# Down and output projections as three 256-column matmuls, with new starting places for weights, memory, x and latents

## The chip, the core and the metric

The kernel runs on one core of one Trainium2 chip. The metric is the device time of one execution in microseconds (us). Before the change it is 1103.97 us, the median of 3 runs (1102.92 to 1104.38).

## What is computed

A trunk of two layers over 256 tokens of width 1024 in float32. Every layer adds to x, in turn, half of a feed-forward network (FFN, width 2816), a mixer, a cross-attention to a memory of 256 tokens, and half of a second FFN. The mixer of the first layer is a differential attention beside a stick-breaking attention (called AB below), that of the second is a latent attention with a low-rank key, value and query (MLA).

```python
def swiglu(h, w_gate, w_up, w_down):
    return (jax.nn.silu(h @ w_gate) * (h @ w_up)) @ w_down
...
        x = x + 0.5 * swiglu(rms_norm(x, ffn_norm[layer, 0]),
                             ffn_w_gate[layer, 0], ffn_w_up[layer, 0], ffn_w_down[layer, 0])
...
            x = x + diff_stickbreak_mixer(h, ab_w_in[i], ab_w_out[i], ...)
...
            x = x + mla_mixer(h, mla_w_dq[i], mla_q_norm[i], mla_w_uq[i], mla_w_dkv[i], ...)
        x = x + memory_cross_attention(rms_norm(x, xm_norm[layer]), rms_norm(mem, xm_mem_norm[layer]), ...)
        x = x + 0.5 * swiglu(rms_norm(x, ffn_norm[layer, 1]), ...)
```

## The kernel before

Every large product is made of numbers that are split in two float32r parts, a high and a low one: high times high, high times low and low times high are added up in one PSUM bank. A matmul of TensorE holds 128x128 numbers (the held operand, loaded by a weight load) and streams the columns of the other operand past them (the streamed operand). In the profile's names `mm<-xh,wh` the first name behind the arrow is the streamed operand, the second the held one.

**Triples and pairs.** `mm3` (line 286) makes a step of 128 rows as three matmuls, lines 287, 288 and 289. `mm2` (line 279) makes it as two: line 282 streams the high and the low part, which lie side by side, as 512 columns past the weight's high part, and line 283 streams the 256 high columns past the weight's low part. The two halves of the bank are then added to x one after the other in `finish_dt` (lines 518 to 520).

```python
        PE.matmul(bank[:, 0:512], w[0], src[2], start=first, stop=False)
        PE.matmul(bank[:, S:512], w[1], src[0], start=False, stop=last)
```

**Which product is which.** Gate and up products (`fm`, line 618), the query projections of the cross-attention, the first projections of MLA and `qb`, `kb` of AB (`fm_g`, line 628) stream x past the weights, as triples. `ka`, `qa`, `va`, `vb` of AB and the memory's keys and values (`tm_g`, line 641) hold x or the memory and stream the weights, as triples of 256 columns; so do `kv_product` (line 1380, 512 columns) and `q_product` (line 1395, 384 columns), which hold the latents. The down products of the FFN (`ffn`, lines 734 to 744) and the output projections of the mixers and the cross-attentions (`out_g`, line 663) are pairs.

**Places.** All sizes of tiles are multiples of 128 bytes. Where an operand starts inside its tile is counted in words of 4 bytes: `COLUMNS` = 28 (112 bytes) and `ROWS` = 36 (144 bytes, 16 past a multiple of 128). x starts at 28 in every stage but AB, where it starts at 36 (`X_AT`, line 72); the hidden activations, the sources of the output projections and the latents at 28 (the slots of the arena, line 185, handed out as a `Pair` of two blocks with a high and a low part each); the memory at 36 (line 790); the weights, loaded in chunks of up to 128x2048, at 0 (line 229).

**Order of the work.** TensorE's order is written by the program itself. In the FFNs it is the order of the loops. In mixers and cross-attentions a planner (`run`, line 438) with estimated times (`spend`, `drop`, `signal`) picks which attention step stands between which pieces of the projections; a product gives way after every 4 steps (lines 635 and 649). A weight chunk is loaded by a DMA on SP's queue, rounded to its high part by ScalarE (line 244), and the low part is subtracted by VectorE, in the mixers a quarter of it by GpSimd (line 246). Three chunks have room (`HL`), so the next chunk's rounding waits until TensorE has left the buffer. The order on the other engines is a scheduler's.

Of the kernel before, what the change touches and what calls it, by code (L numbers as in the profile page):

```python
# [19 lines left out]
P = 128  # L20
S = 256
# [31 lines left out]
WTIME = 4.41  # L53
SLOTS_MLA = (29, 12)
AB_ORDER = ('ka', 'qa', 'vb', 'va', 'k0', 'k1', 'v0')
# [13 lines left out]

COLUMNS, ROWS = 28, 36  # L70

X_AT = (COLUMNS, ROWS) + 7 * (COLUMNS,)
SLOTS_MIX = (29, 12)

# [85 lines left out]
def trunk_kernel(ctx, tc, wflat, xT_d, xtok_d, memT_d, memtok_d, gains_d, rows_d, cst_d, out_d):  # L160
# [109 lines left out]
    def weight(key, n):  # L270
# [6 lines left out]
        return (hi[:, :w].rearrange("p (k n) -> p k n", n=n), lo[:, :w].rearrange("p (k n) -> p k n", n=n))  # L277

    def mm2(bank, w, src, first, last):


        PE.matmul(bank[:, 0:512], w[0], src[2], start=first, stop=False)  # L282
        PE.matmul(bank[:, S:512], w[1], src[0], start=False, stop=last)  # L283
        spend(0.231 + 0.118)

# [203 lines left out]

    class Pair:  # L490


        def __init__(self):
            self.t = alloc("r")
            self.v = self.t.rearrange("p (q h s) -> p q h s", h=2, s=S)
            self.h, self.l = self.v[:, :, 0, :], self.v[:, :, 1, :]
            self.blocks = [(self.v[:, q, 0, :], self.v[:, q, 1, :], self.t[:, q * 512:(q + 1) * 512])
                           for q in range(2)]

# [163 lines left out]
    def out_g(keyf, nchunk, groups, gc):  # L663
# [5 lines left out]
        def part(dt, g):  # L669
# [3 lines left out]
            for i, k in enumerate(rows_):  # L673
                mm2(pss[dt], (w[0][:, k, j * P:(j + 1) * P], w[1][:, k, j * P:(j + 1) * P]),
                    src[i], g == 0 and i == 0, g == len(groups) - 1 and i == len(rows_) - 1)
            if g == len(groups) - 1:
                left[dt // per] -= 1
                if not left[dt // per]:
                    done(keyf(dt // per))
                ps = pss.pop(dt)  # L680
                finish_dt(dt, gc, ps)
                drop(ps, 1.2)

# [12 lines left out]
    def ffn(l, j, gc, need_rb, mem=None):  # L696
# [4 lines left out]
        for f in range(FT // 2):  # L701
# [23 lines left out]
            V.tensor_tensor(out=u, in0=u, in1=s, op=ALU.mult)  # L725
            h = Pair()
            split1(h.h, h.l, u.rearrange("p (a b) -> p a b", b=S))
            rel(u, s)
            tiles.append(h.t)
            hs += h.blocks  # L730
            if mem is not None and f in MEM_AT:
                mem_gain(mem, MEM_AT.index(f))
        begin_phase()
        for dp in range(4):
            pss = [ps_("mm"), ps_("mm")]
            for g0, gn in FF_GROUPS:
                w = weight(("down", l, j, dp, g0), 256)
                for q in range(2):
                    for i in range(gn):
                        k = g0 + i  # L740
                        mm2(pss[q], (w[0][:, i, q * P:(q + 1) * P], w[1][:, i, q * P:(q + 1) * P]),
                            hs[k], k == 0, k == FT - 1)
            for q in range(2):
                finish_dt(dp * 2 + q, gc, pss[q], 0.5)
        rel(*tiles)
# [115 lines left out]
    def cross(l, gc):  # L861
# [32 lines left out]
        def attend(hp):  # L894
# [28 lines left out]
            rel(*pT)  # L923
            h = Pair()
            split1(h.h, h.l, po.rearrange("p (a b) -> p a b", b=S))
            tiles.append(h.t)
            srcs[hp] += h.blocks
            drop(po, 1.3)
# [24 lines left out]
    def mixer_ab(gc):  # L953
# [7 lines left out]

        def add_src(i, h):
            tiles.append(h.t)
            srcs[i] += h.blocks

# [77 lines left out]
        def stick(hq, g):  # L1043
# [12 lines left out]
            for z in zs:  # L1056
# [8 lines left out]
                rel(e)  # L1065
                pr = Pair().t
                split1(pr[:, 0:384], pr[:, 512:896], sp[:, 0:384])
                sps.append((sp, pr))
            for i, (z, (sp, pr)) in enumerate(zip(zs, sps)):
                yield dict(lat=EST_AB['st2'] if i else EST_AB['st1'])  # L1070
                for o in (0, 512):
                    PE.matmul(z[:, 0:384], ntri, pr[:, o:o + 384], start=False, stop=False, skip_group_check=True)
                PE.matmul(z[:, P:S], nones, sp[:, S:384], start=False, stop=True, skip_group_check=True)
# [5 lines left out]
                ws.append(w_)  # L1079
                rel(sp, pr)  # L1080
            yield dict(lat=EST_AB['sto'], o=1 - g, after=[ev["vb", hq]] + [ev["po", hq]] * g)
# [10 lines left out]
            if g == 1:  # L1092
                h = Pair()
                split1(h.h, h.l, po.rearrange("p (a b) -> p a b", b=S))
                add_src(hq, h)
                drop(po, 1.3)
# [94 lines left out]
        def turn_o(g):  # L1191
            yield dict(t=1, after=[ev["oa", t] for t in range(2)])
            pt = transpose4([oa[t][:, (2 * g + j) * P:(2 * g + j + 1) * P] for j in range(2) for t in range(2)])
            h = Pair()
            split(h.h, h.l, pt.rearrange("p (a b) -> p a b", b=S), gsub)
            add_src(2 + g, h)
            drop(pt, 1.4)
# [11 lines left out]
    def mixer_mla(gc):  # L1209
        xg, rs = st.xg, st.rs  # L1210
        ev = defaultdict(Event)
        lat_tiles, tiles, srcs = [], [], [[] for _ in range(4)]
        lat = {"ckv": ([], []), "cq": ([], [])}
        rl, kk, kf, vt, kT, qf, rqs = {}, {}, {}, {}, {}, {}, {}

        def latent(key, gc0, ps):
            pairs, sqs = lat[key]
            h = Pair()
            for j in range(2):
                split(h.blocks[j][0], h.blocks[j][1], ps[:, j * S:(j + 1) * S], gcol(gc0 + j))  # L1220
            pairs += h.blocks
            lat_tiles.append(h.t)
            sq = al()
# [156 lines left out]
        def kv_product(hf):  # L1380
            yield dict(w=("ukv", hf))
            w = weight(("ukv", hf), 1024)
            for t in range(2):
                yield dict(mm=2)
                pk, pv = take("mm"), take("mm")
                for pz, c0 in ((pk, 0), (pv, 512)):
                    for k in range(2):
                        mm3(pz, tuple(z[:, t * P:(t + 1) * P] for z in lat["ckv"][0][k][:2]),
                            (w[0][:, k, c0:c0 + 512], w[1][:, k, c0:c0 + 512]), k == 0, k == 1)
# [17 lines left out]
        def attend(n):  # L1407
# [57 lines left out]
            rel(*pT)  # L1465
            h = Pair()
            split1(h.h, h.l, po.rearrange("p (a b) -> p a b", b=S))
            tiles.append(h.t)
            srcs[n] += h.blocks
            drop(po, 1.3)  # L1470
# [126 lines left out]
```

## Time and profile before

| what | value |
|---|---|
| median of 3 runs (lowest to highest) | 1103.97 us (1102.92 to 1104.38) |
| the profiled execution: its time, its span | 1103.84 us, 1102.1 us |
| TensorE: matmuls, weight loads (busy, share of the span) | 1079.7 us (98%), 1019.4 us (92%) |
| VectorE, ScalarE, GpSimd busy | 793.3 us (72%), 654.9 us (59%), 196.1 us (18%) |
| mean granted clock of TensorE | 0.995 |
| DMA queue of the weights | 191.86 MB, 50.4% of 16 engines |

Matmuls follow each other in a pipeline: one that is listed with 0.28 us may be followed by the next 0.11 us later, so what a matmul costs is read from the distance of two starts, not from its duration. The profile's span runs from the first to the last instruction; the time holds 1.74 us more.

### The profile page before, as it was taken

How to read it: one execution, taken by the hardware profiler on the slowest of the kernel's cores; microseconds unless marked ns; L12 is line 12 of the kernel's file. 1: busy time of each engine (PE TensorE's matmuls, PEld its weight loads, DVE VectorE, ACT ScalarE, POOL GpSimd, SP SyncE). 2: the span in 40 equal slices, each digit the busy share in tenths (PEclk: the TensorE clock that was granted, in tenths of full speed). 3: DMA queues.
4: the chain of work that ended last, by engine and by line, in shares of the span. 5: the costliest groups of instructions: out<-in, count | busy, mean ns of one | idle time of the engine just before them, and what ended most of it. 6: DMA issues, size and time to landing. Idle time of an engine off the chain costs nothing.

```text
span 1102.1 us, 21671 instructions
## 1 busy us (share of the span) xinstructions
PE 1079.7 (98%) x8144; PEld 1019.4 (92%) x8144; DVE 793.3 (72%) x1930; ACT 654.9 (59%) x1775; POOL 196.1 (18%) x210
## 2 busy tenths in 40 slices
PE   8999999999999999999999999999989999999998
PEld 8999988998889899998899999889878899999987
DVE  6888766667877878775777777665678768877653
ACT  6666555576756666554556655565866556655541
POOL 2000001366344200000100000114861422000000
PEclk9999999999999999999999999999989999999999
DMA  8766555535236165545556555554241443655561
GB/s 296 250 236 207 186 172 195 189 106 175 97 123 218 71 229 200 192 182 194 185 183 233 196 207 182 175 190 162 96 138 54 153 146 124 230 193 190 193 218 49
DMA packets 50794, 193.25 MB, mean 175 GB/s; under 512 B 5760, under 2 KB 7552, under 8 KB 35584
## 3 DMA queue, kind: packets, MB, share of 16 engines
q1 hardware_dynamic: 50688, 191.86, 50.4%
q8 instruction: 64, 1.05, 0.4%
q14 instruction: 42, 0.34, 0.1%
HBM read 190.79 MB, written 1.05 MB: 174 GB/s over the span
## 4 chain that ended last, share of the span: by engine, by line
PE 87%; DVE 6%; ACT 3%; POOL 2%; issue 1%; DMA 1%; SPq 0%; DVEq 0%; ACTq 0%; POOLq 0%
PE mm L282 19%; PE mm L287 18%; PE mm L288 18%; PE mm L289 18%; PE mm L283 10%; DVE wl L246 2%; ACT slotf L763 1%; PE t L776 1%; POOL sm L468 1%; PE s L1428 1%; DMA wr<-wflat 1%; PE t L476 1%; PE s L901 0%; PE o L1461 0%; DMA gains<-gains 0%
## 5 line engine op out<-in xcount | busy, mean ns | idle before, releaser
L244 ACT CAST wh<-wr 128x256 fp32r<-128x256 f32 (+1 forms) x1216 | 441.0, 434 | 303.9 <-PE mm L288 141.5
L246 DVE TENSOR_TENSOR wl<-wr,wh 128x256 fp32r<-128x256 f32 (+1 forms) x1171 | 483.6, 466 | 122.5 <-ACT wh L244 111.5
L287 PE MATMUL mm<-xh,wh 128*128 128x256 f32 x1584 | 439.6, 278 | 4.1 <-DVE slotf L715 2.0
L289 PE MATMUL mm<-xh,wl 128*128 128x256 f32 x1584 | 437.6, 276 | 0.1
L288 PE MATMUL mm<-xl,wh 128*128 128x256 f32 x1584 | 437.3, 276 | 0.2 <-DVE xl L483 0.2
L282 PE MATMUL mm<-slotr,wh 128*128 128x512 f32 x896 | 318.3, 398 | 1.1 <-DVE slotr L483 1.1
L287 PEld LDWEIGHTS mm<-xh,wh 128*128 128x128 f32 x1584 | 298.2, 188 | 5.3 <-issue 2.2
L288 PEld LDWEIGHTS mm<-xl,wh 128*128 128x128 f32 x1584 | 298.1, 188 | 0.5 <-DVE xl L483 0.4
L289 PEld LDWEIGHTS mm<-xh,wl 128*128 128x128 f32 x1584 | 298.1, 188 | 0.5 <-DVE wl L267 0.3
L283 PE MATMUL mm<-slotr,wl 128*128 128x256 f32 x896 | 252.2, 281 | 0.0
L282 PEld LDWEIGHTS mm<-slotr,wh 128*128 128x128 f32 x896 | 168.3, 188 | 42.8 <-DVE slotr L483 1.4
L283 PEld LDWEIGHTS mm<-slotr,wl 128*128 128x128 f32 x896 | 168.8, 188 | 0.1
L540 POOL TENSOR_TENSOR acc<-acc,sq 128x256 f32<-128x256 f32 x49 | 42.9, 875 | 462.4 <-ACT sq L532 458.5
L246 POOL TENSOR_TENSOR wl<-wr,wh 128x512 fp32r<-128x512 f32 x45 | 66.8, 1485 | 108.6 <-ACT wh L244 108.6
L723 DVE TENSOR_TENSOR slotf<-mm,rb 128x512 f32<-128x512 f32 x44 | 30.3, 689 | 52.7 <-PE mm L289 52.6
L519 DVE SCALAR_TENSOR_TENSOR x<-mm,x 128x256 f32<-128x256 f32 x128 | 52.1, 416 | 21.4 <-PE mm L283 21.0
L482 ACT ACTIVATE xh<-x,gains 128x256 fp32r<-128x256 f32 x64 | 32.1, 507 | 33.9 <-DVE x L519 29.5
L763 ACT ACTIVATE slotf<-s,sm,sl 128x256 f32<-128x256 f32 (+1 forms) x64 | 32.8, 522 | 23.3 <-DVE sm L757 17.8
L715 DVE TENSOR_TENSOR slotf<-mm,rb 128x512 f32<-128x512 f32 x44 | 30.3, 688 | 20.9 <-PE mm L289 20.8
L483 DVE SCALAR_TENSOR_TENSOR xl<-x,gains,xh 128x256 fp32r<-128x256 f32 x64 | 39.2, 617 | 5.2 <-ACT xh L482 5.2
L287 PE MATMUL mm<-wh,mem 128*128 128x256 f32 x128 | 38.0, 297 | 0.0
L488 DVE TENSOR_TENSOR slotr<-slotf,slotr 128x512 fp32r<-128x512 f32 (+1 forms) x52 | 35.5, 686 | 3.2 <-ACT slotr L487 2.9
(194 smaller groups left out, 1085.5 us busy)
## 6 DMA issues: line engine op xcount, KB each, us to landing
wr<-wflat SPq DMA_DIRECT2D x118, 1024.0 KB, 4.8
wr<-wflat SPq DMA_DIRECT2D x180, 256.0 KB, 3.9
wr<-wflat SPq DMA_DIRECT2D x16, 768.0 KB, 4.4
slotf<-memT SPq DMA_DIRECT2D x8, 256.0 KB, 3.5
x<-xT SPq DMA_DIRECT2D x4, 256.0 KB, 5.1
wr<-wflat SPq DMA_DIRECT2D x2, 512.0 KB, 7.2
slotf<-xtok SPq DMA_DIRECT2D x4, 256.0 KB, 7.6
slotf<-memtok SPq DMA_DIRECT2D x4, 256.0 KB, 3.5
```

The source lines that it names most:

```text
L244: A.copy(hi[:, a:b], raw[:, a:b])
L246: e.tensor_tensor(out=lo[:, a:b], in0=raw[:, a:b], in1=hi[:, a:b].bitcast(F32), op=ALU.subtract)
L282: PE.matmul(bank[:, 0:512], w[0], src[2], start=first, stop=False)
L283: PE.matmul(bank[:, S:512], w[1], src[0], start=False, stop=last)
L287: PE.matmul(out, a[0], b[0], start=first, stop=False, **kw)
L288: PE.matmul(out, a[0], b[1], start=False, stop=False, **kw)
L289: PE.matmul(out, a[1], b[0], start=False, stop=last, **kw)
L483: V.scalar_tensor_tensor(out=lo, in0=src, scalar=g, in1=hi.bitcast(F32), op0=ALU.mult, op1=ALU.subtract))
L488: V.tensor_tensor(out=lo, in0=src, in1=hi.bitcast(F32), op=ALU.subtract)
L519: V.scalar_tensor_tensor(out=xd, in0=ps[:, h * S:(h + 1) * S], scalar=factor, in1=xd, op0=ALU.mult, op1=ALU.add)
L540: G.tensor_tensor(out=st.acc, in0=st.acc, in1=sq, op=ALU.add)
L763: A.activation(p[:, i * w:(i + 1) * w], sps[:, i * w:(i + 1) * w], AF.Exp, bias=nb[:, i:i + 1], scale=r, accum_out=sums[:, i:i + 1])
```

## The change

Three things are done together.

1. `mm2` and `Pair` are gone: down products and output projections are made by `mm3`, from a high and a low part that lie in two slots of 512 words, into 256 columns of a bank. `finish_dt` adds one block to x instead of two.
2. Where the weights are streamed, they start at 28 instead of 0, and what is held (x in AB, the memory, the latents) starts at 0 instead of 36 or 28. In `qb` and `kb`, where x of AB is streamed, x is at 0 instead of 36 and the weights at 56 (224 bytes) instead of 0. All weight buffers get 64 words more.
3. The arenas of the two mixers have 11 slots of 512 words in place of 6 pairs of two. The latents take the first 6.

```diff
-COLUMNS, ROWS = 28, 36
-X_AT = (COLUMNS, ROWS) + 7 * (COLUMNS,)
-SLOTS_MIX = (29, 12)
+COLUMNS = 28
+X_AT = (COLUMNS, 0) + 7 * (COLUMNS,)
+W_COLUMNS = {"ka": 28, "qa": 28, "va": 28, "vb": 28, "memk0": 28, "memv0": 28, "memk1": 28, "memv1": 28,
+             "uq": 28, "ukv": 28, "qb": 56, "kb": 56}
+SLOTS_MIX = (29, 11)
...
-            rows = pool.tile([P, n32r // 2 * 1024 + 64], F32R, name=nm("slotr"))
-            ar["r"] = [rows[:, COLUMNS + i * 1024:COLUMNS + (i + 1) * 1024] for i in range(n32r // 2)]
+            ar["rows"] = pool.tile([P, n32r * 512 + 64], F32R, name=nm("slotr"))
+            ar["r"] = [ar["rows"][:, COLUMNS + i * 512:COLUMNS + (i + 1) * 512] for i in range(n32r)]
...
-        return (raw, *(T(n, [P, width], HL, F32R, wpool) for n in ("wh", "wl")))
+        o = W_COLUMNS.get(key[0], 0)
+        return (raw, *(T(n, [P, width + 64], HL, F32R, wpool)[:, o:o + width] for n in ("wh", "wl")))
...
-                for h in range(2):
-                    V.scalar_tensor_tensor(out=xd, in0=ps[:, h * S:(h + 1) * S], scalar=factor, in1=xd,
-                                           op0=ALU.mult, op1=ALU.add)
+                V.scalar_tensor_tensor(out=xd, in0=ps, scalar=factor, in1=xd, op0=ALU.mult, op1=ALU.add)
...
-                mm2(pss[dt], (w[0][:, k, j * P:(j + 1) * P], w[1][:, k, j * P:(j + 1) * P]),
+                mm3(pss[dt][:, 0:S], (w[0][:, k, j * P:(j + 1) * P], w[1][:, k, j * P:(j + 1) * P]),
...
-                        mm2(pss[q], (w[0][:, i, q * P:(q + 1) * P], w[1][:, i, q * P:(q + 1) * P]),
+                        mm3(pss[q][:, 0:S], (w[0][:, i, q * P:(q + 1) * P], w[1][:, i, q * P:(q + 1) * P]),
...
-    mem_rows = cpool.tile([P, 8 * 512 + 64], F32R, name="mem")
-    mem_hl = [mem_rows[:, ROWS + i * 512:ROWS + (i + 1) * 512] for i in range(8)]
+    mem_rows = cpool.tile([P, 8 * 512], F32R, name="mem")
+    mem_hl = [mem_rows[:, i * 512:(i + 1) * 512] for i in range(8)]
...
+        lat_tiles = [alr() for _ in range(6)]
+        lat_rows = [ar["rows"][:, i * 512:(i + 1) * 512] for i in range(6)]
```

TensorE, the passage from the last up product of the first FFN (`mm_1796`) to its first down product (`mm_1849`), before and then with the change:

```order
L287 MATMUL mm_1796<-xh,wh_1633 128x256
L288 MATMUL mm_1796<-xl,wh_1633 128x256
L289 MATMUL mm_1796<-xh,wl_1634 128x256
L282 MATMUL mm_1849<-slotr_113,wh_1706 128x512
L283 MATMUL mm_1849<-slotr_113,wl_1707 128x256
```

```order
L286 MATMUL mm_1796<-xh,wh_1633 128x256
L287 MATMUL mm_1796<-xl,wh_1633 128x256
L288 MATMUL mm_1796<-xh,wl_1634 128x256
L286 MATMUL mm_1849<-slotr_113,wh_1706 128x256
L287 MATMUL mm_1849<-slotr_113,wh_1706 128x256
L288 MATMUL mm_1849<-slotr_113,wl_1707 128x256
```

The triples keep their order with line numbers one lower, and each pair has become a triple of the same kind.

VectorE, the end of the second pair of column blocks of the same down product (`x` is the sum, `xl` the low part for the next stage, `wl` the low part of the next weights), before and then with the change:

```order
L246 TENSOR_TENSOR wl_2112<-wr_2110,wh_2111 128x256 x6
L519 SCALAR_TENSOR_TENSOR x<-mm_2008,x 128x256
L246 TENSOR_TENSOR wl_2112<-wr_2110,wh_2111 128x256
L519 SCALAR_TENSOR_TENSOR x<-mm_2008,x 128x256
L246 TENSOR_TENSOR wl_2112<-wr_2110,wh_2111 128x256
L483 SCALAR_TENSOR_TENSOR xl<-x,gains,xh 128x256
L519 SCALAR_TENSOR_TENSOR x<-mm_2009,x 128x256
L246 TENSOR_TENSOR wl_2172<-wr_2170,wh_2171 128x256
L519 SCALAR_TENSOR_TENSOR x<-mm_2009,x 128x256
L246 TENSOR_TENSOR wl_2172<-wr_2170,wh_2171 128x256 x3
L483 SCALAR_TENSOR_TENSOR xl<-x,gains,xh 128x256
```

```order
L252 TENSOR_TENSOR wl_2186<-wr_2184,wh_2185 128x256 x6
L510 SCALAR_TENSOR_TENSOR x<-mm_2050,x 128x256
L252 TENSOR_TENSOR wl_2186<-wr_2184,wh_2185 128x256 x2
L482 SCALAR_TENSOR_TENSOR xl<-x,gains,xh 128x256
L510 SCALAR_TENSOR_TENSOR x<-mm_2051,x 128x256
L252 TENSOR_TENSOR wl_2256<-wr_2254,wh_2255 128x256 x2
L482 SCALAR_TENSOR_TENSOR xl<-x,gains,xh 128x256
```

One of two additions per column block is gone, and the second block's low part stands behind two subtractions where it stood behind four.

ScalarE at the same place (`xh` is the high part for the next stage, `sq` its square for the norm, `wh` the high part of the next weights), before and then with the change:

```order
L244 CAST wh_2111<-wr_2110 128x256 x8
L482 ACTIVATE xh<-x,gains 128x256
L532 ACTIVATE sq_2158<-x 128x256
L244 CAST wh_2171<-wr_2170 128x256 x5
L482 ACTIVATE xh<-x,gains 128x256
L532 ACTIVATE sq_2165<-x 128x256
```

```order
L250 CAST wh_2185<-wr_2184 128x256 x8
L481 ACTIVATE xh<-x,gains 128x256
L522 ACTIVATE sq_2243<-x 128x256
L250 CAST wh_2255<-wr_2254 128x256 x2
L481 ACTIVATE xh<-x,gains 128x256
L522 ACTIVATE sq_2249<-x 128x256
```

The second block's activation has moved ahead of three roundings of the weights.

## Rows read from the trace of the kernel before

**Rows 1.** The page's busy times (engine, us, share of the span, instructions).

```profile
PE 1079.7 (98%) x8144; PEld 1019.4 (92%) x8144; DVE 793.3 (72%) x1930; ACT 654.9 (59%) x1775; POOL 196.1 (18%) x210
...
PEclk9999999999999999999999999999989999999999
```

**Rows 2.** The page's chain of work that ended last, by engine.

```profile
PE 87%; DVE 6%; ACT 3%; POOL 2%; issue 1%; DMA 1%; SPq 0%; DVEq 0%; ACTq 0%; POOLq 0%
```

**Rows 3.** Waits, all engines: who waited for whom, us, times, longest.

```profile
ACT wh L244 <- PE mm L288: 141.5, 62, 4.6
...
ACT wh L244 <- PE mm L282: 96.4, 32, 3.7
```

**Rows 4.** Groups of matmuls by line and shape: count, busy us, mean ns.

```profile
L287 PE MATMUL mm<-xh,wh 128*128 128x256 f32 x1584 | 439.6, 278 | 4.1 <-DVE slotf L715 2.0 <-ACT wh L266 1.1 <-ACT wh L244 1.0
...
L282 PE MATMUL mm<-slotr,wh 128*128 128x512 f32 x896 | 318.3, 398 | 1.1 <-DVE slotr L483 1.1
...
L287 PE MATMUL mm<-wh,mem 128*128 128x256 f32 x128 | 38.0, 297 | 0.0
L287 PE MATMUL mm<-wh,xh 128*128 128x256 f32 x128 | 37.5, 293 | 0.0
...
L287 PE MATMUL mm<-wh,slotr 128*128 128x384 f32 x32 | 11.7, 367 | 0.0
...
L287 PE MATMUL mm<-wh,slotr 128*128 128x512 f32 x16 | 6.4, 399 | 0.0
```

**Rows 5.** Timeline of TensorE, gate product: start us, duration, instruction.

```profile
100.06 0.28 PE L287 MATMUL mm<-xh,wh 128*128 128x256 f32 x1
...
103.80 0.28 PE L287 MATMUL mm<-xh,wh 128*128 128x256 f32 x1
```

**Rows 6.** Timeline of TensorE, down product of the second FFN.

```profile
514.73 0.40 PE L282 MATMUL mm<-slotr,wh 128*128 128x512 f32 x1
514.96 0.28 PE L283 MATMUL mm<-slotr,wl 128*128 128x256 f32 x1
...
520.02 0.40 PE L282 MATMUL mm<-slotr,wh 128*128 128x512 f32 x1
```

**Rows 7.** Timeline of TensorE, from the output projection into the cross-attention's query projection.

```profile
335.96 0.28 PE L287 MATMUL mm<-xh,wh 128*128 128x256 f32 x1
...
336.91 0.28 PE L289 MATMUL mm<-xh,wl 128*128 128x256 f32 x1
...
337.93 0.28 PE L289 MATMUL mm<-xh,wl 128*128 128x256 f32 x1
```

**Rows 8.** Timeline of TensorE in AB: x streamed from place 36.

```profile
205.00 0.28 PE L288 MATMUL mm<-xl,wh 128*128 128x256 f32 x1
...
207.85 0.28 PE L288 MATMUL mm<-xl,wh 128*128 128x256 f32 x1
```

**Rows 9.** Timeline of TensorE in AB: weights streamed past x.

```profile
232.08 0.28 PE L287 MATMUL mm<-wh,xh 128*128 128x256 f32 x1
...
236.03 0.28 PE L287 MATMUL mm<-wh,xh 128*128 128x256 f32 x1
```

**Rows 10.** Timeline of TensorE in MLA: weights streamed past a latent, 384 columns.

```profile
786.05 0.34 PE L287 MATMUL mm<-wh,slotr 128*128 128x384 f32 x1
...
789.25 0.34 PE L287 MATMUL mm<-wh,slotr 128*128 128x384 f32 x1
```

**Rows 11.** Stretches: busy PE, PEld, DVE, ACT, POOL, then granted clock, DMA share, GB/s.

```profile
400.00:470.00 70.00, 70.00 (x620) 70.00 (x620) 53.52 (x133) 40.62 (x119) 0.00 (x0) 1.00 0.57 203
130.00:186.00 56.00, 56.00 (x333) 49.20 (x332) 37.14 (x100) 29.92 (x91) 5.04 (x5) 1.00 0.52 184
189.00:331.00 142.00, 136.51 (x1070) 128.73 (x1070) 99.51 (x187) 89.49 (x202) 65.63 (x60) 1.00 0.43 139
739.00:858.00 119.00, 112.13 (x778) 100.86 (x778) 83.93 (x205) 78.47 (x183) 59.73 (x66) 0.97 0.36 117
```

**Rows 12.** Timeline of all engines, the end: the last two additions.

```profile
1098.36 0.88 DVE L519 SCALAR_TENSOR_TENSOR x<-mm,x 128x256 f32<-128x256 f32 x2 [1.24 <-PE mm L283]
```

**Rows 13.** The page's costliest groups, the additions to x.

```profile
L519 DVE SCALAR_TENSOR_TENSOR x<-mm,x 128x256 f32<-128x256 f32 x128 | 52.1, 416 | 21.4 <-PE mm L283 21.0
```

More of the change, by code (lines that the diff above doesn't have):

```diff
@@ L53 @@
 WTIME = 4.41
-SLOTS_MLA = (29, 12)
+SLOTS_MLA = (29, 11)
 AB_ORDER = ('ka', 'qa', 'vb', 'va', 'k0', 'k1', 'v0')
@@ L196, in al, with alr @@
         return alloc("f")
+    def alr():
+        return alloc("r")
     def rel(*ts):
@@ L277, in weight @@
         return (hi[:, :w].rearrange("p (k n) -> p k n", n=n), lo[:, :w].rearrange("p (k n) -> p k n", n=n))
[L279 to L284, printed above, removed]
     def mm3(out, a, b, first, last, **kw):
@@ L488, in split1, with rpair @@
         V.tensor_tensor(out=lo, in0=src, in1=hi.bitcast(F32), op=ALU.subtract)
[L490 to L498, printed above, removed]
+    def rpair():
+        return alr(), alr()
     class State:
@@ L646, in tm_g @@
             for k in range(KT):
-                a = tuple(z[:, t * P:(t + 1) * P] for z in xg[k][:2])
+                a = tuple(z[:, t * P:(t + 1) * P] for z in xg[k])
                 mm3(ps[:, t * S:(t + 1) * S], a, (w[0][:, k, :], w[1][:, k, :]), k == 0, k == KT - 1)
@@ L680, in part @@
                 ps = pss.pop(dt)
-                finish_dt(dt, gc, ps)
-                drop(ps, 1.2)
+                finish_dt(dt, gc, ps[:, 0:S])
+                drop(ps, 0.8)
         nw = BANKS["mm"]
@@ L725, in ffn @@
             V.tensor_tensor(out=u, in0=u, in1=s, op=ALU.mult)
-            h = Pair()
-            split1(h.h, h.l, u.rearrange("p (a b) -> p a b", b=S))
+            hh, hl = rpair()
+            split1(hh, hl, u)
             rel(u, s)
-            tiles.append(h.t)
-            hs += h.blocks
+            tiles += [hh, hl]
+            for q in range(2):
+                hs.append((hh[:, q * S:(q + 1) * S], hl[:, q * S:(q + 1) * S]))
             if mem is not None and f in MEM_AT:
@@ L923, in attend @@
             rel(*pT)
[L924 to L927, printed above, removed]
+            hh, hl = rpair()
+            split1(hh, hl, po)
+            tiles.extend([hh, hl])
+            srcs[hp] += [(hh[:, j * S:(j + 1) * S], hl[:, j * S:(j + 1) * S]) for j in range(2)]
             drop(po, 1.3)
@@ L960, in mixer_ab, with add_src @@
         raw = {}
-        def add_src(i, h):
-            tiles.append(h.t)
-            srcs[i] += h.blocks
+        def add_src(i, hh, hl):
+            tiles.extend([hh, hl])
+            srcs[i] += [(hh[:, j * S:(j + 1) * S], hl[:, j * S:(j + 1) * S]) for j in range(2)]
         def products():
@@ L1065, in stick @@
                 rel(e)
[L1066 to L1069, printed above, removed]
+                hh, hl = rpair()
+                split1(hh[:, 0:384], hl[:, 0:384], sp[:, 0:384])
+                sps.append((sp, hh, hl))
+            for i, (z, (sp, hh, hl)) in enumerate(zip(zs, sps)):
                 yield dict(lat=EST_AB['st2'] if i else EST_AB['st1'])
-                for o in (0, 512):
-                    PE.matmul(z[:, 0:384], ntri, pr[:, o:o + 384], start=False, stop=False, skip_group_check=True)
+                for h_ in (hh, hl):
+                    PE.matmul(z[:, 0:384], ntri, h_[:, 0:384], start=False, stop=False, skip_group_check=True)
                 PE.matmul(z[:, P:S], nones, sp[:, S:384], start=False, stop=True, skip_group_check=True)
@@ L1079, in stick @@
                 ws.append(w_)
-                rel(sp, pr)
+                rel(sp, hh, hl)
             yield dict(lat=EST_AB['sto'], o=1 - g, after=[ev["vb", hq]] + [ev["po", hq]] * g)
@@ L1092, in stick @@
             if g == 1:
-                h = Pair()
-                split1(h.h, h.l, po.rearrange("p (a b) -> p a b", b=S))
-                add_src(hq, h)
+                hh, hl = rpair()
+                split1(hh, hl, po)
+                add_src(hq, hh, hl)
                 drop(po, 1.3)
@@ L1193, in turn_o @@
             pt = transpose4([oa[t][:, (2 * g + j) * P:(2 * g + j + 1) * P] for j in range(2) for t in range(2)])
-            h = Pair()
-            split(h.h, h.l, pt.rearrange("p (a b) -> p a b", b=S), gsub)
-            add_src(2 + g, h)
+            hh, hl = rpair()
+            split(hh, hl, pt, gsub)
+            add_src(2 + g, hh, hl)
             drop(pt, 1.4)
@@ L1211, in mixer_mla @@
         ev = defaultdict(Event)
-        lat_tiles, tiles, srcs = [], [], [[] for _ in range(4)]
+        tiles, srcs = [], [[] for _ in range(4)]
+        lat_tiles = [alr() for _ in range(6)]
+        lat_rows = [ar["rows"][:, i * 512:(i + 1) * 512] for i in range(6)]
         lat = {"ckv": ([], []), "cq": ([], [])}
@@ L1217, in latent @@
             pairs, sqs = lat[key]
-            h = Pair()
+            hh, hl = lat_rows.pop(0), lat_rows.pop(0)
             for j in range(2):
-                split(h.blocks[j][0], h.blocks[j][1], ps[:, j * S:(j + 1) * S], gcol(gc0 + j))
-            pairs += h.blocks
-            lat_tiles.append(h.t)
+                sl_ = slice(j * S, (j + 1) * S)
+                split(hh[:, sl_], hl[:, sl_], ps[:, sl_], gcol(gc0 + j))
+                pairs.append((hh[:, sl_], hl[:, sl_]))
             sq = al()
@@ L1387, in kv_product @@
                     for k in range(2):
-                        mm3(pz, tuple(z[:, t * P:(t + 1) * P] for z in lat["ckv"][0][k][:2]),
+                        mm3(pz, tuple(z[:, t * P:(t + 1) * P] for z in lat["ckv"][0][k]),
                             (w[0][:, k, c0:c0 + 512], w[1][:, k, c0:c0 + 512]), k == 0, k == 1)
@@ L1401, in q_product @@
                 for k in range(4):
-                    mm3(ps[:, 0:384], tuple(z[:, t * P:(t + 1) * P] for z in lat["cq"][0][k][:2]),
+                    mm3(ps[:, 0:384], tuple(z[:, t * P:(t + 1) * P] for z in lat["cq"][0][k]),
                         (w[0][:, k, :], w[1][:, k, :]), k == 0, k == 3)
@@ L1465, in attend @@
             rel(*pT)
[L1466 to L1469, printed above, removed]
+            hh, hl = rpair()
+            split1(hh, hl, po)
+            tiles.extend([hh, hl])
+            srcs[n] += [(hh[:, j * S:(j + 1) * S], hl[:, j * S:(j + 1) * S]) for j in range(2)]
             drop(po, 1.3)
```

2 lines of the change are left out of this document (1 added, 1 removed).

## The prediction

> **What bounds the kernel now.** I read the busy times first: TensorE is busy 98% of the span and no other engine over 72% [rows 1]. The chain of waits says the same with more right, since it follows what was waited for: 87% of it is TensorE [rows 2]. The waits turn it round: ScalarE, which makes the weights ready, stood 141.5 us and 96.4 us waiting for TensorE to leave a buffer [rows 3], so the weights are early and TensorE is late. By stretches, gate and up products and down products fill TensorE wholly (70.00 of 70.00 us, 56.00 of 56.00 us), the mixers nearly: AB leaves it idle 5.5 us of 142, MLA 6.9 us of 119 [rows 11]. So the time is a count of matmuls times their distance, and the question is that distance. Busy times and mean durations don't tell it, as 278 ns are listed for matmuls that follow each other faster [rows 4]; I take it from starts in the timeline.
>
> - Gate: 33 matmuls from 100.06 to 103.80 us, 113.3 ns each, a triple 340.0 ns [rows 5].
> - Down: 15 pairs from 514.73 to 520.02 us, 352.7 ns a pair [rows 6].
> - x streamed from place 36: 24 in 2.85 us, 118.75 ns, a triple 356.3 ns [rows 8].
> - Weights streamed from place 0 past x at 36: 33 in 3.95 us, 119.7 ns, a triple 359.1 ns [rows 9].
>
> One shape, 256 columns, has three prices, and the cheapest belongs to streamed operand at 28, held operand at 0. A passage adds something: after the pairs of an output projection the first eight matmuls take 0.95 us (118.75 ns each), the next nine 1.02 us (113.3 ns), in the same place and shape [rows 7]. So 113.3 ns is a repeating rhythm that a run of equal matmuls falls into after about eight; where x was at 36, the 24 matmuls above never did.
>
> **The change, part by part.** The profiled execution took 1103.84 us, 0.13 us under the median; the sum is made against it.
>
> *Down products.* Pairs become triples of the gate's form, with the same starting places (28 and 0). There are 4 FFNs x 8 column blocks x 22 steps = 704 of the 896 [rows 4], in four unbroken runs of 528 matmuls, so the slow first eight don't count. 352.7 - 340.0 = 12.7 ns a step: 704 x 12.7 = **8.9 us** less, all on the path. Weights must now come every 16 x 0.340 = 5.44 us; that is the gate's pace, which the gate holds with TensorE full [rows 11].
>
> *Output projections.* The other 192 steps, at most 2.4 us; attention work breaks them into runs that each begin slowly. I take **2.1 us**.
>
> *Weights streamed past x and memory.* 128 + 128 triples [rows 4] go from 0 past 36 to 28 past 0, the gate's places: 359.1 - 340.0 = 19.1 ns, 4.9 us at most. Two things take from it: products give way after every four steps, and eight slow matmuls in a run of 24 cost a third; and in AB and MLA TensorE already waits at times for attention steps, which come no earlier for having the product done sooner. Ends 0 and 4.9 us; I take the middle, **2.5 us**.
>
> *qb and kb.* x goes to 0, the weights that it passes to 56: no row has this pair of places. Bounds for 64 triples: 340.0 ns (1.0 us less) and 359.1 ns (0.2 us more). The nearest row is x at 16 past a multiple of 128 bytes [rows 8], so **nothing**.
>
> *Latents held at 0, weights at 28.* The 384-column matmuls take 3.20 us for 18, 177.8 ns [rows 10]; at the gate's rate per column 170.0 ns, so 96 x 7.8 = 0.75 us at most. The 512-column ones (16 triples) at most twice the gap between 118.75 and 113.3 ns, 48 x 10.9 = 0.5 us. Between 0 and 1.3 us I take **0.3 us**, since these runs are short.
>
> *One addition to x in place of two.* 64 of 128 go, at 416 ns [rows 13]: 26.6 us of VectorE's work, which lies beside TensorE. On the path is the end alone, where two additions (0.88 us) follow the last matmul [rows 12]: **0.4 us**. The freed place moves the second block's activation on ScalarE ahead of three roundings, so it may stand there for x while roundings queue behind it, and TensorE waits for those last. The cover is ScalarE's idle time, 26 of 56 us in the down stretch, and VectorE's, 19 of 56 [rows 11]; without it each of the 16 ends of two blocks could cost TensorE one addition, 0.4 us.
>
> *Slots.* 11 single slots for 6 pairs change when a slot comes free, not TensorE's order, which stays but for four transposes moved by two steps near the end of MLA: nothing. The DMAs are the same in number and order.
>
> The sum: 8.9 + 2.1 + 2.5 + 0 + 0.3 + 0.4 = 14.2 us less, **1089.6 us**.
>
> **The rivals.**
>
> *The place is not what matters.* If 113.3 ns is gate's for another reason (its weights lie block after block, the down weights in rows twice as wide), down and output steps run like those first eight: 356.3 ns, 3.6 ns over a pair, 896 x 3.6 = 3.2 us more; nothing else gains but the end: 1103.84 + 3.2 - 0.4 = **1106.6 us**. It decides from 352.7 / 3 = 117.6 ns a matmul on: above that three lose to two. For it: line 283 streams from 28 past 0 too and never comes down from 0.12 us (352.7 ns less the 0.23 us from 514.73 to 514.96) [rows 6]. Against it: there every second matmul has 512 columns, so no run of equal ones can form, and a run needs eight [rows 7]; x from 28 and x from 36 differ by the place alone [rows 5, 8]. The Trainium skill (TensorE: Matmul & The Clock Gate, section Back-to-back issue gap) knows no place at all: a warm matmul takes its columns at 2.4 GHz plus 2.5 ns, so a pair 325.0 ns and a triple 327.5 ns, and the change would make the kernel 2.2 us slower. By the same page (section Step-by-step: what each phase is for) loading the next weights takes nothing from the running matmul's reads. The rows disagree with the first on size, 113.3 to 119.7 ns where it has 109.2, and neither explains three prices for one shape, so I go by the rows.
>
> *The gate loses its rhythm.* The wider weight tiles move every tile behind them; if 113.3 ns hangs on distances between tiles and not on places within 128 bytes, the other 1520 triples of the 1584 [rows 4] go to 356.3 ns: 24.8 us more, and with the 3.2 us above **1131 us**. Against it: in the gate x's high and low part are in two tiles and weights step from block to block, all at different distances, at one price [rows 5].
>
> *The mixers give it back.* An attention step that comes late opens a new wait, long enough that the clock falls: MLA, with granted clock 0.97 where the others have 1.00 [rows 11], has one such stretch already, worth 0.03 x 119 = 3.6 us. Then the 2.8 us of the mixers are lost and 3.6 us added: **1096 us**.
>
> **How the numbers follow.** The forecast has 0.83, the first rival 0.07, the second 0.03, the third 0.07. The range's low end is all terms at their full size: 8.9 + 2.4 + 4.9 + 1.0 + 1.3 + 0.4 = 18.9 us, 1085 us. The high end, 1095 us, is the down products alone, which have the least doubt. About 0.17 is left outside. A difference of 0.2%, 2.2 us, is about the least that a measurement of this kernel tells from none. Faster: the forecast and the third rival, 0.90. The first rival lies just beyond that bound, so I split its chance: same 0.03, slower 0.04; with the second, slower 0.07.
>
> **What would show it.** Right: in the down stretch starts 113.3 ns apart without a break, 528 in about 59.8 us; the same after the first eight in `ka` to `vb` and in the memory's products; 64 additions to x; gate still at 113.3 ns. Wrong: down matmuls at 118 to 120 ns, gate above 114 ns, or waits of TensorE in AB and MLA that add up to over 15 us.

## The result and the profile after

The changed kernel takes 1088.8 us, median of 4 runs (1087.76 to 1090.49), against 1103.45 us (1101.1 to 1104.38) of the kernel before, measured beside it: ratio 0.9872, 95% interval [0.985, 0.9894]. In a later measurement it was 0.9877 [0.9855, 0.9899]. The forecast was 1089.6 us. The profiled execution took 1090.49 us, its span 1088.8 us.

The page after, busy times, clock, the chain by engine and the group of additions to x:

```profile
PE 1065.9 (98%) x9040; PEld 1046.5 (96%) x9040; DVE 769.4 (71%) x1866; ACT 655.4 (60%) x1775; POOL 192.5 (18%) x210
...
PEclk9999999999999999999999999999989999999999
...
PE 87%; DVE 5%; ACT 2%; POOL 2%; DMA 2%; issue 1%; SPq 0%; DVEq 0%; ACTq 0%; POOLq 0%
...
L510 DVE SCALAR_TENSOR_TENSOR x<-mm,x 128x256 f32<-128x256 f32 x64 | 26.7, 418 | 23.5 <-PE mm L288 23.3
```

TensorE is still busy 98% and 87% of the chain [rows 1, 2], with 896 matmuls more and 13.8 us less. Of 128 additions 64 are left, 25.4 us less work of VectorE [rows 13].

The down product of the second FFN, TensorE's timeline: first matmul of the stage, a stretch in it, and the first gate matmul behind it.

```profile
493.48 0.28 PE L286 MATMUL mm<-slotr,wh 128*128 128x256 f32 x1
...
511.84 0.28 PE L286 MATMUL mm<-slotr,wh 128*128 128x256 f32 x1
511.95 0.28 PE L287 MATMUL mm<-slotr,wh 128*128 128x256 f32 x1
512.07 0.28 PE L288 MATMUL mm<-slotr,wl 128*128 128x256 f32 x1
512.18 0.28 PE L286 MATMUL mm<-slotr,wh 128*128 128x256 f32 x1
...
553.32 0.28 PE L286 MATMUL mm<-xh,wh 128*128 128x256 f32 x1
```

528 matmuls in 59.84 us are 113.3 ns each from the first on: the down product takes the gate's rhythm over without a break. The same stage before, from its first pair to the next gate matmul:

```profile
496.72 0.39 PE L282 MATMUL mm<-slotr,wh 128*128 128x512 f32 x1
...
558.89 0.28 PE L287 MATMUL mm<-xh,wh 128*128 128x256 f32 x1
```

It took 62.17 us, 2.33 us more, 353.2 ns a pair. With such starts the span divides into stages (us, before and after):

| stage | before | after | difference |
|---|---|---|---|
| ahead of the first gate matmul, first gate stage | 134.1 | 135.1 | +1.0 |
| the other three gate stages | 362.1 | 362.4 | +0.3 |
| four down stages, with the end | 252.6 | 242.7 | -9.9 |
| output projections of the mixers | 24.9 + 25.8 | 24.1 + 25.0 | -1.7 |
| output projections of the cross-attentions | 11.6 + 11.6 | 11.1 + 11.1 | -1.1 |
| AB, MLA | 114.8 + 107.6 | 114.0 + 106.4 | -2.1 |
| cross-attentions | 28.4 + 28.4 | 28.6 + 28.4 | +0.1 |

The sum is -13.3 us, the difference of the spans. The first row is no effect of the change: that stage ended between 130.6 and 135.1 us in the profiles below whose gate is the same, and of the changed kernel itself at 135.1 us here and 130.6 us in the later measurement.

The gates' +0.3 comes from the two gate stages that follow an output projection. There TensorE now stands for the low part of x's last block, which VectorE makes after the projection has ended; before, the same step did not stand (its two matmuls below, then those with the change and what they waited for):

```profile
340.76 0.28 PE L287 MATMUL mm<-xh,wh 128*128 128x256 f32 x1
340.88 0.28 PE L288 MATMUL mm<-xl,wh 128*128 128x256 f32 x1
```

```profile
336.91 0.97 DVE L482 SCALAR_TENSOR_TENSOR xl<-x,gains,xh 128x256 fp32r<-128x256 f32 x1
...
337.74 0.28 PE L286 MATMUL mm<-xh,wh 128*128 128x256 f32 x1
...
337.94 0.39 PE L287 MATMUL mm<-xl,wh 128*128 128x256 f32 x1
...
338.16 0.28 PE L288 MATMUL mm<-xh,wl 128*128 128x256 f32 x1
```

The low part is there at 337.88, the matmul on it starts at 337.94, and the next one 0.22 us later. The rows are from the cross-attention's query projection; behind each of the four output projections the two distances are 162 to 198 and 223 to 228 ns in place of 113, some 0.2 us each time.

The end after: the last addition to x, on VectorE.

```profile
1085.62 0.42 DVE L510 SCALAR_TENSOR_TENSOR x<-mm,x 128x256 f32<-128x256 f32 x1 [1.62 <-PE mm L288]
```

One where two took 0.88 us [rows 12]. From its start to the end of the span are 3.2 us, where from the first of the two were 3.7.

In AB, weights streamed past x: the first matmul of a run, the tenth, and one 25 later.

```profile
219.28 0.28 PE L286 MATMUL mm<-wh,xh 128*128 128x256 f32 x1
...
220.35 0.28 PE L286 MATMUL mm<-wh,xh 128*128 128x256 f32 x1
...
223.18 0.28 PE L287 MATMUL mm<-wl,xh 128*128 128x256 f32 x1
```

Nine at 118.7 ns, then 113.3 ns [rows 9: a mean of 119.7]. With the starts of the runs the mean over x and memory is 115.2 ns, where it was 119.4. `qb` and `kb`, x at 0 past weights at 56, are at 116.7 ns: 23 matmuls in 2.68 to 2.69 us.

```profile
207.72 0.28 PE L286 MATMUL mm<-xh,wh 128*128 128x256 f32 x1
...
210.41 0.28 PE L288 MATMUL mm<-xh,wl 128*128 128x256 f32 x1
```

In MLA the 384-column matmuls, held latent at 0, take 2.60 us for 15, 173 ns [rows 10: 177.8 ns]. Before the change half of them already ran at 173 ns, at the same places as those of rows 10: below, ten of them in 1.73 us before, then the 15 after.

```profile
782.73 0.33 PE L288 MATMUL mm<-wl,slotr 128*128 128x384 f32 x1
...
784.46 0.34 PE L289 MATMUL mm<-wh,slotr 128*128 128x384 f32 x1
```

```profile
777.27 0.33 PE L286 MATMUL mm<-wh,slotr 128*128 128x384 f32 x1
...
779.87 0.34 PE L286 MATMUL mm<-wh,slotr 128*128 128x384 f32 x1
```

What the faster matmuls save in AB comes back in part as waiting. AB as a stretch (columns as in [rows 11]) and TensorE's waits in it, before:

```profile
196.20:311.00 114.80, 110.43 (x922) 106.17 (x921) 82.42 (x157) 74.73 (x173) 55.71 (x52) 1.00 0.45 143
```

```profile
PE t L776 <- DVE slotf L836: 1.9, 1, 1.9
PE s L324 <- ACT slotf L763: 1.4, 2, 0.8
PE o L1088 <- issue: 0.8, 1, 0.8
PE o L1088 <- ACT slotf L1000: 0.2, 1, 0.2
```

AB and MLA, and the waits in AB, after:

```profile
194.90:308.90 114.00, 108.05 (x923) 103.58 (x921) 81.12 (x156) 74.54 (x172) 55.63 (x52) 1.00 0.46 144
734.00:840.20 106.20, 99.28 (x702) 90.31 (x701) 75.17 (x190) 71.13 (x170) 56.90 (x64) 0.97 0.37 120
```

```profile
PE t L767 <- DVE slotf L827: 2.2, 1, 2.2
PE s L323 <- ACT slotf L754: 1.9, 2, 1.0
PE o L1079 <- issue: 0.9, 1, 0.9
PE o L1079 <- ACT slotf L991: 0.9, 1, 0.9
```

TensorE is busy 2.4 us less and idle 1.6 us more (4.4 to 6.0); the four waits have grown from 4.3 to 5.9 us. So of 2.4 us the stage kept 0.8. MLA is idle 6.9 us as before, its granted clock 0.97 as before. In the later profile of the changed kernel AB took 113.9 us again, but MLA 107.4 us, so that most of MLA's -1.2 us is not shown to be the change's.

### The profile page after: what moved, and what is told of

Its sections match the earlier page's. It is cut to its first block, busy times and chain, and to the rows that moved or that the text cites. A ratio compares the mean times of both kernels' runs of the same rounds, so it can differ in the third digit from the quotient of the medians.

```text
span 1088.8 us, 23382 instructions
## 1 busy us (share of the span) xinstructions
PE 1065.9 (98%) x9040; PEld 1046.5 (96%) x9040; DVE 769.4 (71%) x1866; ACT 655.4 (60%) x1775; POOL 192.5 (18%) x210
## 4 chain that ended last, share of the span: by engine, by line
PE 87%; DVE 5%; ACT 2%; POOL 2%; DMA 2%; issue 1%; SPq 0%; DVEq 0%; ACTq 0%; POOLq 0%
PE mm L286 28%; PE mm L288 27%; PE mm L287 27%; DVE wl L252 2%; DMA wr<-wflat 2%; ACT slotf L754 1%; PE t L767 1%; POOL sm L467 1%; PE s L1422 1%; PE t L475 1%; PE s L892 0%; PE o L1455 0%; DVE sm L745 0%; ACT wh L250 0%; POOL sl L467 0%
## 5 line engine op out<-in xcount | busy, mean ns | idle before, releaser
L286 PE MATMUL mm<-slotr,wh 128*128 128x256 f32 x896 | 247.6, 276 | 0.3 <-ACT slotr L481 0.3
L287 PE MATMUL mm<-slotr,wh 128*128 128x256 f32 x896 | 246.6, 275 | 0.4 <-DVE slotr L482 0.4
L288 PE MATMUL mm<-slotr,wl 128*128 128x256 f32 x896 | 246.5, 275 | 0.0
L286 PEld LDWEIGHTS mm<-slotr,wh 128*128 128x128 f32 x896 | 168.2, 188 | 1.0 <-ACT slotr L481 0.6
L287 PEld LDWEIGHTS mm<-slotr,wh 128*128 128x128 f32 x896 | 168.2, 188 | 0.7 <-DVE slotr L482 0.6
L530 POOL TENSOR_TENSOR acc<-acc,sq 128x256 f32<-128x256 f32 x49 | 38.7, 790 | 455.0 <-ACT sq L522 452.9
L481 ACT ACTIVATE xh<-x,gains 128x256 fp32r<-128x256 f32 x64 | 32.1, 507 | 29.8 <-DVE x L510 25.8
L510 DVE SCALAR_TENSOR_TENSOR x<-mm,x 128x256 f32<-128x256 f32 x64 | 26.7, 418 | 23.5 <-PE mm L288 23.3
```

The source lines that it names most:

```text
L286: PE.matmul(out, a[0], b[0], start=first, stop=False, **kw)
L287: PE.matmul(out, a[0], b[1], start=False, stop=False, **kw)
L288: PE.matmul(out, a[1], b[0], start=False, stop=last, **kw)
L481: return (A.activation(hi, src, AF.Identity, scale=g), V.scalar_tensor_tensor(out=lo, in0=src, scalar=g, in1=hi.bitcast(F32), op0=ALU.mult ...
L510: V.scalar_tensor_tensor(out=xd, in0=ps, scalar=factor, in1=xd, op0=ALU.mult, op1=ALU.add)
```

## Experiments

The theory: a run of equal matmuls settles in a rhythm whose price hangs on where the streamed and the held operand start. Rivals: the layout of the product decides and not the places; or the places alone decide, and equal lengths are not needed. A time without a ratio is that of a single run.

**The change in two halves.** First the triples alone: places stay as they were.

```diff
-X_AT = (COLUMNS, 0) + 7 * (COLUMNS,)
+X_AT = (COLUMNS, 36) + 7 * (COLUMNS,)
-W_COLUMNS = {"ka": 28, ...}
+W_COLUMNS = {}
...
+    mem_hl = [mem_rows[:, 36 + i * 512:36 + (i + 1) * 512] for i in range(8)]
+        lat_rows = list(lat_tiles)
```

> The kernel before with the first part of the change alone: triples in place of pairs, all places as before. My theory (streamed at 28 past held at 0 lets a run of equal matmuls fall into 113.3 ns): down starts 113.3 ns apart, 896 steps x 12.7 ns = 11.4 us less, about 1092 us, while weights streamed past x stay at 119.7 ns. Rival (the triples are quick only together with the new places or the wider weight tiles): down at 118 to 120 ns, 1103 to 1109 us.

1091.46 us, ratio 0.9916 [0.9899, 0.9932]. Down stages take 59.8 us as with the whole change, weights streamed past x stay at 119.6 ns, AB takes 114.7 and MLA 107.8 us.

Then the places alone: pairs stay.

```diff
-X_AT = (COLUMNS, ROWS) + 7 * (COLUMNS,)
+X_AT = (COLUMNS, 0) + 7 * (COLUMNS,)
+W_COLUMNS = {"ka": 28, ...}
...
+    mem_hl = [mem_rows[:, i * 512:(i + 1) * 512] for i in range(8)]
+        lat_rows = [ar["rows"][:, i * 1024:(i + 1) * 1024] for i in range(3)]
```

> The kernel before with the second part alone: new places of weights, memory, x and latents, pairs kept. My theory: products that stream weights fall to 113.3 ns after some eight matmuls of each run, 2.5 to 4 us less, 1099.5 to 1101 us; the pairs stay at 352.7 ns. Rival (the mixers wait for their attention steps and give all of it back): 1103 to 1104 us.

1100.61 us, ratio 0.9989 [0.9977, 1.0001]: not told apart from no change. In its trace the places do their work all the same: weights streamed past x or memory at 115.0 to 115.3 ns, AB 113.9 us, MLA 106.9 us, down 62.2 us as before. So nearly all of the gain is the triples', and in the mixers the places are worth 0.8 to 0.9 us in AB, by either half. In MLA it is 0.8 to 1.4, which the spread of that stage (106.4 and 107.4 us in two profiles of the changed kernel) does not tell from less.

**Why a pair was dear.** The pairs' own layout, places and bank halves, but the 512 columns cut in two.

```diff
-        PE.matmul(bank[:, 0:512], w[0], src[2], start=first, stop=False)
+        PE.matmul(bank[:, 0:S], w[0], src[0], start=first, stop=last, skip_group_check=True)
+        PE.matmul(bank[:, S:512], w[0], src[1], start=False, stop=False, skip_group_check=True)
```

> The kernel before with line 282's 512 columns cut into two matmuls of 256 into the two halves of the bank; pairs' layout, two additions and places as before. My theory (unequal lengths kept the pairs out of the rhythm): 113.3 ns a matmul, 11 to 12 us less, about 1092 us. Rival (the side by side layout or the second half of the bank costs it): 118 to 120 ns, 1103 to 1109 us.

1092.96 us. A down stretch of it, 49 matmuls apart:

```profile
514.36 0.28 PE L282 MATMUL mm<-slotr,wh 128*128 128x256 f32 x1
...
519.91 0.28 PE L283 MATMUL mm<-slotr,wh 128*128 128x256 f32 x1
```

113.3 ns: neither layout nor bank halves kept the pairs from the rhythm, the matmul of 512 columns did. The 1092.96 us hold the old places in the mixers and both additions; they lie within the range of the triples alone (1088.99 to 1093.0 us), which hold the old places too.

Whether its length or the alternation of two lengths is at fault was not tried apart, but the changed kernel has a row on it: in MLA 24 equal matmuls of 512 columns stream from 28 past 0.

```profile
759.73 0.39 PE L286 MATMUL mm<-wh,slotr 128*128 128x512 f32 x1
...
765.03 0.40 PE L288 MATMUL mm<-wh,slotr 128*128 128x512 f32 x1
```

23 in 5.30 us are 230 to 231 ns, and 225, 231 and 237 ns take turns, against 2 x 113.3 = 226.7 ns for the same columns in two. By that, as an estimate, length alone would cost some 4 of the 13 ns that a pair costs over a triple, and the rest goes with the alternation.

Now the triples of the change with their slots at 0, past weights at 0:

```diff
-            ar["r"] = [ar["rows"][:, COLUMNS + i * 512:COLUMNS + (i + 1) * 512] for i in range(n32r)]
+            ar["r"] = [ar["rows"][:, i * 512:(i + 1) * 512] for i in range(n32r)]
```

> The change with the slots of the arena at 0 in place of 28, so that down products and output projections are triples that stream from 0 past 0. My theory (the place makes the rhythm): 118 to 120 ns a matmul, 14 to 20 ns a step over the change, 896 steps, 12 to 18 us more: 1101 to 1107 us. Rival (three equal matmuls are quick wherever they lie): 113.3 ns, 1089 us.

1105.76 us. Its down stretch, 45 matmuls apart:

```profile
514.56 0.28 PE L286 MATMUL mm<-slotr,wh 128*128 128x256 f32 x1
...
519.96 0.28 PE L286 MATMUL mm<-slotr,wh 128*128 128x256 f32 x1
```

120.0 ns, and the stage 63.4 us where pairs took 62.2: at the wrong place three matmuls lose to two. This is the first rival's price, but brought about by the place, which that rival held to be without effect: 112 bytes.

**Which places.** Held operand at 0, the streamed one elsewhere, another place in each stage:

```diff
+X_AT = (4, 0, 20, 8, 12, 24, 26, 16, 28)
...
+    with arena(*SLOTS_FFN, 20):
```

> The change with another starting place of the streamed operand in every stage, held weights at 0 throughout: gate and up of the four FFNs at 4, 8, 12 and 16 words, down of the first FFN at 20, of the second and third at 24, of the fourth at 32. My theory (the place within 128 bytes decides): 32 words costs what 0 does, 120 ns; the others lie between 113 and 120 ns, and only some of them fall into an even rhythm. Rival (28 is quick for another reason, such as the distance between two tiles): no order in them, and 32 differs from 0.

1122.33 us. Places in words: 4 gave 118.7 ns, 8 116.7, 12 118.3, 16 117.8, 20 and 24 120.0, 32 118.7; 26 gave 120.0. Since 32 is not 0's 120.0 (the run before), the pattern doesn't repeat after 128 bytes, and the theory of the place within 128 bytes failed there.

Then streamed at 28, the FFN's weights elsewhere:

```diff
+W_HELD = {("gate", 0, 0): 4, ("gate", 0, 1): 8, ("gate", 1, 0): 16, ("gate", 1, 1): 24,
+          ("down", 0, 0): 28, ("down", 0, 1): 12, ("down", 1, 0): 20, ("down", 1, 1): 32}
```

> The change with another starting place of the held weights in every stage, streamed operand at 28 throughout: gate and up of the four FFNs held at 4, 8, 16 and 24 words, down at 28, 12, 20 and 32. If the distance of the two places decides, held 4 costs what a streamed place of 24 past 0 does in the other kernel, 8 what 20 does, 12 what 16, 16 what 12, 20 what 8, 24 what 4, and 28 costs 120 ns as 0 past 0 does. If only the streamed place decides, all cost 113.3 ns. 32 costs 113.3 ns by both.

1119.6 us. Gate: 4 and 8 gave 120.0 ns, 16 118.3, 24 118.7; down: 28 and 20 118.3, 32 117.2, but 12 113.3. The held place moves the price as much as the streamed one does. The four gate stages cost what the theory of the distance had said, of the down stages none did; 32, which both theories had put at 113.3, missed too.

Then 123 other pairs of places in runs of 36 to 48 matmuls, streamed at odd multiples of 4 words, held at many places:

```diff
+X_AT = (28, 0, 28, 12, 44, 28, 28, 60, 28)
+HOLD = [0, 4, 8, ..., 60, 2, 10, 14, 18, 26, 30]
+HOLD_DOWN = [0, 4, 8, ..., 44]
```

> The change with the streamed operand of gate and up at 28, 12, 44 and 60 words in the four FFNs, of down at 20, 36 and 52, and the held weights at another place in every chunk (0, 4, 8 to 60 and some between). If the even rhythm belongs to a few pairs of places, most chunks cost 116 to 120 ns a matmul and a few 113.3 ns, 28 past 0 and 28 past 12 among them; if both places shifted alike keep the price, 44 past 16, 60 past 32 and 12 past 48 are quick too (16, 32 and -16 words on). A chunk under 113 ns would point to a quicker kernel. About 1115 to 1125 us in all.

1118.18 us. 13 of the 123 settled at 113.3 ns, the other 110 at 116.5 to 120.2, none below 113.3. The 13 are those, and all those, whose distance (streamed less held place, in words, modulo 64) is 28, 48 or 10. Most pairs ran once, so a pair that has two prices would show one of them; streamed 36 past 0, which ran in two FFNs, gave 118.7 ns in one and 116.7 in the other. Two runs of the scan, streamed at 12 past held 52, then past held 2:

```profile
452.94 0.28 PE L297 MATMUL mm<-xh,wh 128*128 128x256 f32 x1
...
457.25 0.28 PE L297 MATMUL mm<-xh,wh 128*128 128x256 f32 x1
...
471.52 0.28 PE L297 MATMUL mm<-xh,wh 128*128 128x256 f32 x1
...
474.58 0.28 PE L297 MATMUL mm<-xh,wh 128*128 128x256 f32 x1
```

36 matmuls in 4.31 us, 119.7 ns; 27 in 3.06 us, 113.3 ns.

**Does the distance suffice?** Three variants in AB. x at 28 for all, so `qb`, `kb` get the gate's places and the weights stream from 28 past 28:

```diff
-X_AT = (COLUMNS, 0) + 7 * (COLUMNS,)
+X_AT = (COLUMNS, COLUMNS) + 7 * (COLUMNS,)
-             "uq": 28, "ukv": 28, "qb": 56, "kb": 56}
+             "uq": 28, "ukv": 28}
```

> The change with x of AB at 28 in place of 0 and the weights of qb and kb at 0 in place of 56. qb and kb then stream from 28 past 0 and fall to 113.3 ns, 64 triples x 3 x 3.4 ns = 0.7 us less; ka to vb stream weights from 28 past x at 28: by the distance theory 120 ns, 128 triples x 3 x 5 ns = 1.9 us more; by the theory of the streamed place alone no change.

1086.24 us, not told apart from the changed kernel's 1086.23 to 1092.64: `qb`, `kb` settle at 113.3 ns where they had 116.7, `ka` to `vb` have a mean of 118.0.

The same, with those weights at 56, so distance 28 again, but from an even multiple of 4 words:

```diff
+W_COLUMNS = {"ka": 56, "qa": 56, "va": 56, "vb": 56, ...
```

> x of AB at 28 as in the run before, and the weights of ka, qa, va, vb at 56, so that they stream from 56 past 28: both places of the quick pair moved by 28 words. If a common shift keeps the price, 113.3 ns once a run has settled; if each place counts by itself, 116 to 120 ns. qb and kb at 113.3 ns in either case.

1088.23 us: `ka` to `vb` have a mean of 119.0 ns, some runs settled at 116.7 and the others at 120.0. A quick distance alone doesn't do. Before the change it was the same: streamed 0, held 36 is distance 28, and cost 119.7 ns [rows 9]. In both the streamed place is an even multiple of 16 bytes, in all quick pairs of the scan an odd one; that this is what decides is not shown.

The same, with those weights at 12, distance 48, and the changed kernel itself beside it:

```diff
+W_COLUMNS = {"ka": 12, "qa": 12, "va": 12, "vb": 12, ...
```

> The changed kernel, but x of AB starts at 28, the weights of ka, qa, va and vb at 12 (they stream past x), those of qb and kb at 0 (x streams past them). Both pairs of places were at 113.3 ns in the scan, though there with x streamed. If the two places decide, whatever the operands are, ka to vb and qb, kb all settle at 113.3 ns: the first as after the change, the second 3 ns a matmul faster, 192 x 3.3 ns = 0.6 us less than the changed kernel in the same call, too little for a measurement. If weights streamed past x behave otherwise than x streamed past weights, ka to vb are at 116.5 to 120 ns and the kernel takes 1 to 2 us more than the changed one.

> The changed kernel itself, beside the variant with other places in AB: a ratio to the kernel before of 0.987, and qb and kb at 116.7 ns a matmul again.

1087.06 us (1085.58 to 1089.5), ratio 0.9856 [0.9842, 0.9871], and the changed kernel 1088.26 us (1086.23 to 1092.64), 0.9877 [0.9855, 0.9899]. `ka` to `vb` and `qb`, `kb` all settle at 113.3 ns, so the scan's pairs hold with weights streamed past x too. Whether this variant beats the changed kernel is not shown: the intervals overlap, and in its profile AB took 114.9 us beside 113.9, with granted clock 0.99 beside 1.00.

**One pair of places, two prices.** Distance 16 gave 118.3 ns in the scan and 113.3 in one down stage. All FFN weights at 12:

```diff
+             "uq": 28, "ukv": 28, "gate": 12, "up": 12, "down": 12, "qb": 56, "kb": 56}
```

> The changed kernel with the FFN weights held at 12 instead of 0, so streamed 28 past held 12 in all gate, up and down products. In the scan this distance of 16 words gave 118.3 ns at every streamed place; in one down stage of the run on held places it gave 113.3 ns over 528 matmuls. If places alone decide, gate and down are all at 118.3 ns: 4560 gate and up matmuls and 2112 down ones, 5 ns each, 33 us more, 1122 us. If the layout of the product matters too (down: high and low part two slots of one tile), gate is at 118.3 and all four down stages at 113.3: 23 us more, 1112 us. If one pair of places has two rhythms and the entry decides, stages of one kind differ among themselves, and the time lies between 1089 and 1122 us.

1109.97 us. Down stage of the third FFN, then of the fourth:

```profile
699.99 0.28 PE L286 MATMUL mm<-slotr,wh 128*128 128x256 f32 x1
...
712.06 0.28 PE L286 MATMUL mm<-slotr,wh 128*128 128x256 f32 x1
...
1060.02 0.28 PE L286 MATMUL mm<-slotr,wh 128*128 128x256 f32 x1
...
1071.24 0.28 PE L286 MATMUL mm<-slotr,wh 128*128 128x256 f32 x1
```

102 matmuls at 118.3 ns, 99 at 113.3. The first three FFNs ran at 118.3 ns but for three runs of 48 at the start of a gate stage and short pieces of the very first, broken one, the fourth at 113.3 but for one such run. Neither the places alone nor the layout explain this: at this distance there are two rhythms, and a run keeps the one that it fell into. The rhythm changed behind a break in the run, in the fourth FFN behind distances of 362 and 306 ns; what makes a run fall into the one or the other was not found. It is not this distance alone either: streamed 36 past 0, 56 past 28 and, before the change, the 384-column matmuls of MLA had two prices at one pair of places as well.

## Why the prediction was right

*Down products* (8.9 us forecast): right in mechanism, 528 matmuls in 59.84 us as forecast. The size is 4 x 2.33 = 9.3 us, since a pair takes 353.2 ns over the whole stage; the 352.7 were read from 15 pairs, 5.29 us between starts rounded to 0.01.

*Output projections* (2.1 us, "at most 2.4"): measured 2.7 us. The step that failed is the reason for taking something off: pairs in broken runs were slow too. In the cross-attentions 32 steps took 11.63 us before and 11.1 after, 364 and 347 ns with all that stands between, so pairs lost 10 ns there to their settled price and triples 7.

*Weights streamed past x and memory, and latents* (2.5 + 0.3 us): mis-sized, 2.0 us for mixers and cross-attentions together. The two deductions were the right ones. Slow starts leave 115.2 of 113.3 ns, and in AB 1.6 of 2.4 us went into waits. The latents' bound of 0.75 us took rows 10 for all of the 384-column matmuls, of which half were at 173 ns already.

*qb and kb* (nothing): 116.7 ns where 118.75 had been taken as the nearest, 0.4 us. It lies within the bounds, and within the 2.0 us.

*End* (0.4 us): 0.6 us, the addition's 0.46 and a shorter wait for the last transfer. *The moved activation* (nothing): no wait of TensorE came at the ends of blocks in the stage shown; its 528 matmuls run through all of them without a break. Behind the output projections, which the term left out, TensorE does wait for the last block, for its low part from VectorE and not for a weight: some 0.2 us four times, in part made good by starts without slow matmuls.

With the first stage's +1.0 and the gates' +0.3, which no term had, the terms give the 13.3 us of the spans: 9.3 + 0.6 (the table's 9.9), 2.7 and 2.0 less, 1.3 more. The forecast's chain of argument held; the closeness of its total, 14.2 us, is in part luck, since misses of opposite signs offset each other.

*The rivals.* The place does matter: the run with the slots at 0 brings the first rival's loss about by the place alone, at 120.0 ns rather than its 356.3 / 3 = 118.75. The gate kept its 113.3 ns. The mixers gave back 1.6 us, not 6.4, and the clock of MLA stayed.

By the formula of the Trainium skill (TensorE: Matmul & The Clock Gate, section Back-to-back issue gap) triples would, as an estimate, have lost 2.2 us against pairs; the runs show 340.0 ns against 353.2, so the measurement decides against it here. The section gives the formula for an isolated matmul and not for a stream of weight loads and matmuls, which the prediction left unsaid. By the Trainium skill (TensorE: Matmul & The Clock Gate, section Step-by-step: what each phase is for) a weight load takes nothing from the streamed operand's reads; the runs show that the held operand's place changes the distance of matmuls, 113.3 to 120.0 ns, without showing what collides.

## What to carry to other kernels

Take the price of a matmul from the distance of starts in a settled stretch, for each pair of starting places, before counting instructions: here three equal matmuls at 113.3 ns beat two unequal ones at 353.2 ns, and at 120.0 ns they lose to them. Where TensorE bounds a kernel and steps interrupt a product, a lower price is worth less than its count, since runs begin slowly and attention steps come no earlier. Copy a pair of places that a trace shows settled, rather than a rule for it.

## What was not expected of the hardware

- The price of a 256-column float32r matmul hangs on the starting places of both operands within 256 bytes: in 123 pairs of places, all streamed from an odd multiple of 16 bytes, 113.3 ns at three distances (112, 192 and 40 bytes) and 116.5 to 120.2 ns at the others.
- At distance 64 bytes both 113.3 and 118.3 ns occur, each kept for hundreds of matmuls, and two prices at one pair of places occur elsewhere too.
- Matmuls of 512 and 256 columns in turn stayed at 353 ns a pair; the same columns in three equal matmuls took 340.0, at the same places. Equal matmuls of 512 columns took 231 ns, more than two of 256.
- Why these distances are quick is open: the runs show the pattern, not the mechanism.
